# Ten of 22 up and gate pairs by seven block products in a fused two-block kernel

## The chip, the cores and the metric

The kernel runs on one core of a Trainium2 chip. The metric is the time of one execution on the device in microseconds (us); the profiler's trace of one execution shows where the time goes.

## What is computed

Two network blocks run one after the other on 512 tokens of width 1024, all in float32. The change lies in the last part, the gated feed-forward network of the second block:

```python
def conv_gated_mlp(xn, w_up_gate, conv_w_ffn, w_down):
    u, g = jnp.split(xn @ w_up_gate, 2, axis=-1)      # w_up_gate: 1024 x 5632
    u = causal_dwconv_2(u, conv_w_ffn)                # 3 taps along the tokens
    return (jax.nn.gelu(u) * g) @ w_down              # w_down: 2816 x 1024
...
        ffn = conv_gated_mlp(rms_norm(h, g_pre_ffn[layer]), w_up_gate[layer],
                             conv_w_ffn[layer], w_down[layer])
        h = h + rms_norm(ffn, g_post_ffn[layer])
```

Sixteen meta tokens stand ahead of the 512. The convolution reaches back two tokens, so u is made for 516 columns (four of them ahead of the 512).

## The kernel before

Matrix products are done in a split form: every float32 operand becomes a rounded part hi (type fp32r) and the rest lo = x - hi, and a product of two 128-deep blocks is three matmuls, hi·hi, hi·lo and lo·hi (`mm3`, L101 to L103). `split` (L77, L78) makes both parts: ScalarE casts to hi, VectorE subtracts. `load_w` (L87) brings one 1024x128 column block of a weight into a raw tile (three buffers, one DMA of 512 KB on SyncE's queue), and `split_w` splits it into `whi` and `wlo` (three buffers). `proj` multiplies one such block with half of the columns of x (258 of 516) over KT = 8 blocks of depth: 24 matmuls into one PSUM bank. Six banks go round for this.

The up projection works through 22 pairs m. A pair is one column block of u (weights at m·128) and the matching one of the gate (weights at 2816 + m·128), each for two halves of the columns: 4 calls of `proj`, 96 matmuls. x is here the residual h times the gain, not yet normed: the factor 1/rms of each token, `rb`, is multiplied in when PSUM is read (VectorE, L1269 for u, L1279 for the gate). Then the three taps of the convolution (VectorE, L1271 and twice L1273), the gelu (ScalarE, L1275) and the product with the gate (GpSimd, L1280) give `act[m]`. In pairs 6 to 13 one eighth of the residual each is loaded (L1255), transposed on TensorE (L1258) and copied to `ht` by VectorE (L1260); in pair 14 the gain `gpb` is loaded (L1284).

Ahead of it ends the mixer: its last projection into `yo`, `post_norm` (L266, L270), which adds to h, and `make_xs` (L82, L207), which makes the split x, `xs`, in two halves of columns; h lies in tiles of the ring `yc`. Behind it the down projection splits `act[k]` and the rows of w_down and runs 24 matmuls of 512 columns for each of 22 k into all eight banks.

Each engine has one queue and works it in order. What stands in it first is not set by the code's order alone: a planner sorts the instructions of each engine by a simulated time when the program is built, and a buffer that is taken again waits for its last reader. Pools with `reuse_waits="tile"` wait tile by tile for the memory of a released pool.

## Time and profile before

| | us |
|---|---|
| median of 3 runs | 1978.87 (1978.68 to 1979.2) |
| profiled execution, its own time | 1978.26 |
| its span in the trace | 1976.5 |
| up projection in the trace | 1584 to 1848 |
| mean granted clock of TensorE, of full speed | 0.998 |

The span is from the first to the last recorded instruction; about 1.8 us lie around it. PE is TensorE (matmuls; PEld its weight loads), DVE VectorE, ACT ScalarE, POOL GpSimd, SP SyncE, whose queue SPq issues the DMAs. Matmuls are pipelined: a recorded matmul lasts longer than the distance to the next, so the number of matmuls in a stretch, or the distance of two evictions, tells more than the busy time. In square brackets behind a row stands the idle time of the engine before it and what ended it.

### The profile page before, as it was taken

To read this page: it belongs to the slowest core of one execution; us is meant where nothing else is said; L and a number is where in the kernel's file an instruction comes from. 1 tells how busy PE (TensorE), PEld (TensorE's weight loads), DVE (VectorE), ACT (ScalarE), POOL (GpSimd) and SP (SyncE) were. 2 spreads that over 40 slices of the span, in tenths; PEclk is the share of its full clock that TensorE was granted. 3 is DMA by queue.
4 is the path that set the end of the run, shared out by engine and by line. 5 is a ranking of instruction groups with operands and counts; after the bars stand their busy time and mean duration, and the time that the engine had idled before them with its cause. 6 is when DMAs were issued, how large, how long until landed. Compare 5 with 4: busy or idle time off the path is not lost.

```text
span 1976.5 us, 33284 instructions
## 1 busy us (share of the span) xinstructions
PE 1953.6 (99%) x13398; PEld 1800.3 (91%) x13398; DVE 1267.4 (64%) x2143; ACT 973.5 (49%) x1839; POOL 246.1 (12%) x315
## 2 busy tenths in 40 slices
PE   8999999999999999999999999999999999999998
PEld 6999988888899888888899999999999999999886
DVE  6667677778672566664897878787344485655533
ACT  5555567768655633354756555555222452222322
POOL 1111000000030011100531212120001031111000
PEclk9999999999999999999999999999999999999999
DMA  6223322222433333333221222222333443332332
GB/s 179 67 79 88 86 76 75 75 65 86 144 110 106 95 89 89 92 133 118 88 65 55 65 65 65 58 68 81 92 94 93 149 126 99 102 102 86 96 96 75
DMA packets 260665, 181.37 MB, mean 92 GB/s; under 512 B 8866, under 2 KB 245631, under 8 KB 260511
## 3 DMA queue, kind: packets, MB, share of 16 engines
q1 hardware_dynamic: 259455, 179.21, 30.4%
q8 instruction: 105, 1.72, 0.4%
q14 instruction: 49, 0.40, 0.1%
q10 hardware_dynamic: 1056, 0.04, 0.0%
HBM read 168.59 MB, written 10.63 MB: 91 GB/s over the span
## 4 chain that ended last, share of the span: by engine, by line
PE 92%; DVE 4%; ACT 2%; POOL 1%; DMA 1%; issue 1%; DVEq 0%; POOLq 0%; ACTq 0%; SPq 0%
PE ps L103 17%; PE ps L101 17%; PE ps L102 17%; PE ps_v L103 5%; PE ps_v L102 5%; PE ps_v L101 5%; PE ps_o L101 3%; PE ps_o L102 3%; PE ps_o L103 3%; PE ps_d L101 2%; PE ps_d L103 2%; PE ps_d L102 2%; PE ps_z L1026 1%; PE ps_o L1103 1%; DVE yo L266 1%; DVE h L270 1%
## 5 line engine op out<-in xcount | busy, mean ns | idle before, releaser
L102 PE MATMUL ps<-xl,whi 128*128 128x258 f32 (+3 forms) x2112 | 656.0, 311 | 3.1 <-DVE xl L82 2.9
L101 PE MATMUL ps<-xh,whi 128*128 128x258 f32 (+3 forms) x2112 | 653.7, 313 | 1.0 <-ACT xh L81 0.9
L103 PE MATMUL ps<-xh,wlo 128*128 128x258 f32 (+3 forms) x2112 | 654.8, 311 | 0.0
L77 ACT CAST whi<-wraw 128x1024 fp32r<-128x1024 f32 (+2 forms) x315 | 314.5, 1004 | 454.1 <-PE ps L102 263.4
L78 DVE TENSOR_TENSOR wlo<-wraw,whi 128x1024 fp32r<-128x1024 f32 (+2 forms) x315 | 390.5, 1245 | 183.5 <-ACT whi L77 181.8
L102 PEld LDWEIGHTS ps<-xl,whi 128*128 128x128 f32 x2112 | 400.0, 189 | 28.0 <-DVE xl L82 4.9
L101 PEld LDWEIGHTS ps<-xh,whi 128*128 128x128 f32 x2112 | 397.3, 189 | 24.8 <-ACT xh L81 1.7
L103 PEld LDWEIGHTS ps<-xh,wlo 128*128 128x128 f32 x2112 | 399.3, 189 | 22.2
L101 PE MATMUL ps_v<-whi,xh 128*128 128x256 f32 x896 | 254.5, 286 | 3.5 <-ACT xh L81 3.1
L103 PE MATMUL ps_v<-whi,xl 128*128 128x256 f32 x896 | 253.6, 285 | 1.4 <-DVE xl L82 1.1
L102 PE MATMUL ps_v<-wlo,xh 128*128 128x256 f32 x896 | 254.1, 284 | 0.0
L101 PEld LDWEIGHTS ps_v<-whi,xh 128*128 128x128 f32 x896 | 169.6, 190 | 6.3 <-ACT xh L81 4.6
L103 PEld LDWEIGHTS ps_v<-whi,xl 128*128 128x128 f32 x896 | 170.0, 190 | 3.4 <-DVE xl L82 2.6
L102 PEld LDWEIGHTS ps_v<-wlo,xh 128*128 128x128 f32 x896 | 170.5, 190 | 1.5 <-DVE wlo L78 0.2
L103 PE MATMUL ps<-hi,wlo 128*128 128x258 f32 x384 | 108.7, 284 | 0.0
L101 PE MATMUL ps<-hi,whi 128*128 128x258 f32 x384 | 107.7, 282 | 0.0
L102 PE MATMUL ps_o<-xl,whi 128*128 128x512 f32 x192 | 75.7, 394 | 0.0
L101 PE MATMUL ps_o<-xh,whi 128*128 128x512 f32 x192 | 75.3, 395 | 0.0
L103 PE MATMUL ps_o<-xh,wlo 128*128 128x512 f32 x192 | 74.3, 394 | 0.0
L103 PEld LDWEIGHTS ps<-hi,wlo 128*128 128x128 f32 x384 | 72.7, 189 | 0.0
L101 PEld LDWEIGHTS ps<-hi,whi 128*128 128x128 f32 x384 | 72.4, 189 | 0.0
L103 PE MATMUL ps_d<-whi,xl 128*128 128x512 f32 x176 | 69.3, 394 | 0.0
(533 smaller groups left out, 3427.7 us busy)
## 6 DMA issues: line engine op xcount, KB each, us to landing
wraw<-in_l_w_in_dram SPq DMA_DIRECT2D x112, 512.0 KB
wraw<-in_w_in_dram SPq DMA_DIRECT2D x64, 512.0 KB
wraw<-in_w_up_gate_dram SPq DMA_DIRECT2D x44, 512.0 KB
wraw<-in_l_w_out_dram SPq DMA_DIRECT2D x24, 512.0 KB
wraw<-in_w_down_dram SPq DMA_DIRECT2D x22, 512.0 KB
wraw<-in_l_w_out_dram SPq DMA_DIRECT2D x16, 256.0 KB
wraw<-in_w_proj_attn_dram SPq DMA_DIRECT2D x8, 512.0 KB
wraw<-in_w_proj_conv_dram SPq DMA_DIRECT2D x8, 512.0 KB
```

What stands on the lines that cost most here:

```text
L77: A.copy(hi, src)
L78: V.tensor_tensor(lo, src, hi.bitcast(F32), op=ALU.subtract)
L101: T.matmul(ps, lhsT=ah, rhs=bh, start=first, stop=False, **kw)
L102: T.matmul(ps, lhsT=ah, rhs=bl, start=False, stop=False, **kw)
L103: T.matmul(ps, lhsT=al, rhs=bh, start=False, stop=last, **kw)
L266: mult = (G if i % 4 == 3 else V).tensor_tensor(yo[i][:, c], yo[i][:, c], r[:, c], op=ALU.mult)
L270: add_ = V.tensor_tensor(hs, hs, yo[i][:, c], op=ALU.add)
L1026: T.matmul(ps, lhsT=m_, rhs=x_[:, c0:c0 + n], start=False, stop=False, **kw)
L1103: T.matmul(po[:, n0:], lhsT=l_[:, b, hh:hh + 2, :].rearrange("p a d -> p (a d)"), rhs=a_[r_][:, c0:c0 + S - n0], start=po_first[0], stop=F ...
```

## The change

For ten of the pairs 6 to 21 the four products (u and gate, two halves of the columns) are computed as one 2x2 block product by seven products: the depth is cut into two halves of 4 blocks (HK), the weights into u and gate, x into its two halves of columns. `seven_w` loads both raw weights and forms the sums of blocks on VectorE (`sa`, `sb`), splits r1 whole (products 1 and 2), `sb` (6 and 3), `sa` (5 and 7) and the second half of r2 (4). `seven_x` forms, once for all pairs, the blocks and sums of x; because sums over columns and depth can't be normed afterwards by one factor, x is normed first (`xn` = h · gain · rb), in four steps within the pairs 0 to 3. `seven` runs the products, lets some add onto the bank of an earlier one, copies partial sums out by ScalarE (`keep`) and evicts u and the gate on VectorE with the additions left. The six other pairs of 6 to 21 are `plain`, with splits of the same normed x, u copied out by ScalarE, the gate multiplied with the gelu as it is evicted. The order from pair 6 on is SSPSSPSPSSPSSPSP (S by seven products). Pairs 0 to 5 stay as they were.

With it: the first tap of the convolution goes to ScalarE in all pairs; the product of gate and gelu goes from GpSimd to VectorE in the seven-product pairs; the copies of the residual go to ScalarE and into freed tiles of `xs`, in pairs 8 to 15; h gets tiles of its own (`hr`); `gpb` and the last splits of w_down are in a pool (`fd`) over the memory of the normed x, and gpb is loaded behind pair 21.

```diff
...
         T.matmul(ps, lhsT=ah, rhs=bh, start=first, stop=False, **kw)
         T.matmul(ps, lhsT=ah, rhs=bl, start=False, stop=False, **kw)
         T.matmul(ps, lhsT=al, rhs=bh, start=False, stop=last, **kw)
+    HK = KT // 2
+    kw = dict(skip_group_check=True)
+    def seven_w(pool, w, c1, c2):
+        lo, hi = slice(0, HK), slice(HK, KT)
+        r1 = load_w(w, 0, KT, c1, 128)
+        r2 = load_w(w, 0, KT, c2, 128)
+        sb = pool.tile([128, KT, 128], F32, tag="sb", name="sb", bufs=1)
+        sa = pool.tile([128, KT, 128], F32, tag="sa", name="sa", bufs=1)
+        w_ = {}
+        def put(names, *sp_):
+            for i, nm in enumerate(names):
+                w_[nm] = [x_[:, i * HK:(i + 1) * HK] for x_ in sp_]
+        put("12", *split_w(r1))
+        V.tensor_tensor(sa[:, lo], r2[:, lo], r2[:, hi], op=ALU.add)
+        V.tensor_tensor(sb[:, lo], sa[:, lo], r1[:, lo], op=ALU.add)
+        V.tensor_tensor(sb[:, hi], sb[:, lo], r1[:, hi], op=ALU.add)
+        put("63", *split_w(sb))
+        V.tensor_tensor(sa[:, hi], r1[:, lo], r2[:, lo], op=ALU.add)
+        put("57", *split_w(sa))
+        four = [pool.tile([128, HK, 128], F32R, tag=f"four{r}", name="four", bufs=1) for r in "hl"]
+        split(r2[:, hi], *four)
+        put("4", *four)
+        return w_
+    def seven_x(pool, tmp, p, xa, xb, n, out):
+        tq = tmp.tile([128, 4, n], F32, tag="tq", name="tq", bufs=2)
+        h0, h1 = slice(0, n), slice(n, 2 * n)
+        t1, t2, t3, t4 = (tq[:, i] for i in range(4))
+        V.tensor_tensor(t1, xa[:, h0], xa[:, h1], op=ALU.subtract)
+        V.tensor_tensor(t3, xa[:, h1], xb[:, h1], op=ALU.subtract)
+        V.scalar_tensor_tensor(t2, xb[:, h1], -1.0, t1, op0=ALU.mult, op1=ALU.subtract)
+        V.tensor_tensor(t4, xb[:, h0], t2, op=ALU.add)
+        for src, names in ((xa, "10"), (xb, "23"), (tq.rearrange("p a b -> p (a b)"), "5674")):
+            sp_ = [pool.tile([128, n * len(names)], F32R, tag=f"sx{names}{r}{p}", name=f"sx{r}") for r in "hl"]
+            split(src, *sp_)
+            for i, nm in enumerate(names):
+                out[nm, p] = [x_[:, i * n:(i + 1) * n] for x_ in sp_]
+    def seven(sw, sx, n, snap, o11, o12, o21, o22):
+        bank = {}
+        def product(nm, b, start):
+            if start:
+                bank[b] = pst("mm", n, f"ps_s{b}")
+            wh, wl = sw[nm]
+            for k in range(HK):
+                mm3(bank[b], wh[:, k], wl[:, k], *sx[nm, k], start and k == 0, k == HK - 1, **kw)
+            return bank[b]
+        def keep(ps):
+            t_ = next(snap)
+            A.copy(t_, ps)
+            return t_
+        s1 = keep(product("1", "x", True))
+        V.tensor_tensor(o11, product("2", "y", True), s1, op=ALU.add)
+        v2 = keep(product("6", "x", False))
+        s7 = keep(product("7", "w", True))
+        x5 = product("5", "x", False)
+        v4 = keep(x5)
+        n22, n21 = o22.shape[1], o21.shape[1]
+        V.tensor_tensor(o22, s7[:, n - n22:], x5[:, n - n22:], op=ALU.subtract)
+        V.tensor_tensor(o12, product("3", "z", True), v4, op=ALU.add)
+        V.tensor_tensor(o21, product("4", "w", False)[:, n - n21:], v2[:, n - n21:], op=ALU.subtract)
+    def plain(wt, sx, n, half, c0=0):
+        ps = pst("mm", n - c0)
+        wh, wl = wt
+        for k in range(KT):
+            xh, xl = sx[("10", "23")[k // HK][half], k % HK]
+            mm3(ps, wh[:, k, :], wl[:, k, :], xh[:, c0:], xl[:, c0:], k == 0, k == KT - 1)
+        return ps
     def w_cols(w, c0, n, fine=None):
...
         mo = tc.alloc_tile_pool(name="mo", bufs=1, reuse_waits="tile")
         mg = list(split_into("of", part))
         yo = [mx.tile([128, NQ], F32, tag=f"part{i}", name=f"yo{i}") for i in range(KT)]
-        h[:] = [ring("yc") for i in range(KT)]
+        hr = tc.alloc_tile_pool(name="hr", bufs=1, side="right", reuse_waits="tile")
+        h[:] = [hr.tile([128, NQ], F32, tag=f"h{i}", name=f"h{i}") for i in range(KT)]
         for i in range(KT):
             nc.sync.dma_start(h[i], hd[i][:, Q0:])
         acc, acc2 = new_acc(), new_acc()
...
     banks(mm=(2, 3, 4, 5, 6, 7), at=(0, 1))
     load_set(SET_GELU, "bc")
     with ExitStack() as ff:
-        fp = ff.enter_context(tc.tile_pool(name="fp", bufs=2))
-        act = [fp.tile([128, S], F32, tag=f"act{i}", name=f"act{i}", bufs=1) for i in range(22)]
-        gpb = fp.tile([128, D], F32, tag="gpb", name="gpb", bufs=1)
-
-        ht = [fp.tile([128, D], F32, tag=f"ht{t}", name=f"ht{t}", bufs=1) for t in range(4)]
+        fp = ff.enter_context(tc.tile_pool(name="fp", bufs=2, reuse_waits="tile"))
+        FIRST = 6
+        act = [fp.tile([128, S], F32, tag=f"act{i}", name=f"act{i}", bufs=1) for i in range(FIRST)]
+        wu = a["w_up_gate_2"][0]
+        def conv_gelu(m, u):
+            cv = fp.tile([128, S], F32, tag="cv", name="cv")
+            A.activation(cv, u[:, 4:], AF.Copy, scale=pv("conv_w_ffn_2", 44 + m))
+            for tp in (1, 2):
+                V.scalar_tensor_tensor(cv, u[:, 4 - tp:NQ - tp], pv("conv_w_ffn_2", (2 - tp) * 22 + m), cv,
+                                       op0=ALU.mult, op1=ALU.add)
+            last["gelu"] = A.activation(cv, cv, AF.Gelu_apprx_tanh)
+            return cv
+        fx = tc.alloc_tile_pool(name="fx", bufs=1, reuse_waits="tile")
+        ft = tc.alloc_tile_pool(name="ft", bufs=1, side="right", reuse_waits="tile")
+        sx = {}
+        for m in range(FIRST):
+            wt = split_w(load_w(wu, 0, KT, m * 128, 128))
+            u = fp.tile([128, NQ], F32, tag="u", name="u")
+            for i in range(2):
+                ps = proj(wt, xs, i * HQ, HQ)
+                V.tensor_tensor(u[:, i * HQ:(i + 1) * HQ], ps, rb[:, i * HQ:(i + 1) * HQ], op=ALU.mult)
+            cv = conv_gelu(m, u)
+            wt = split_w(load_w(wu, 0, KT, FF + m * 128, 128), parts=1 if m else 4)
+            for c0, c1 in ((4, HQ), (HQ, NQ)):
+                ps = proj(wt, xs, c0, c1 - c0)
+                V.tensor_tensor(act[m][:, c0 - 4:c1 - 4], ps, rb[:, c0:c1], op=ALU.mult)
+            G.tensor_tensor(act[m], act[m], cv, op=ALU.mult)
+            xn = []
+            for i in (m, m + HK) if m < HK else ():
+                xn.append(ft.tile([128, NQ], F32, tag="xn", name="xn", bufs=2))
+                V.scalar_tensor_tensor(xn[-1], h[i], pv("g_pre_ffn_2", i), rb[:, :NQ], op0=ALU.mult, op1=ALU.mult)
+            if xn:
+                seven_x(fx, ft, m, *xn, HQ, sx)
+        ft.release()
+        hr.release()
+        fa = tc.alloc_tile_pool(name="fa", bufs=1, side="right", reuse_waits="tile")
+        act += [fa.tile([128, S], F32, tag=f"act{i}", name=f"act{i}") for i in range(FIRST, 22)]
+        fw = tc.alloc_tile_pool(name="fw", bufs=1, side="right", reuse_waits="tile")
+        free = [xsp.tile([128, L2], F32, tag="xs", name="fr") for _ in range(16)]
+        ht = [[free[2 * t + i][:, :S] for i in range(2)] for t in range(4)]
+        hls = itertools.cycle([x_[:, :S] for x_ in free[8:10]])
+        snap = itertools.cycle([x_[:, c:c + HQ] for x_ in free[10:] for c in (0, HQ)])
         def residual(i):
-            hl = fp.tile([128, S], F32, tag="hl", name="hl")
+            hl = next(hls)
             nc.sync.dma_start(hl, hd[i][:, META:])
             ps = pst("at", S, "ps_h")
             for t in range(4):
                 T.transpose(ps[:, t * 128:(t + 1) * 128], hl[:, t * 128:(t + 1) * 128], ident)
             for t in range(4):
-                V.tensor_copy(ht[t][:, i * 128:(i + 1) * 128], ps[:, t * 128:(t + 1) * 128])
-
-        wu = a["w_up_gate_2"][0]
-        uw, gw = w_cols(wu, 0, FF), w_cols(wu, FF, FF, 1)
-        for m in range(22):
-            wt = next(uw)
+                A.copy(ht[t][i // 4][:, i % 4 * 128:(i % 4 + 1) * 128], ps[:, t * 128:(t + 1) * 128])
+        for m in range(FIRST, 22):
             u = fp.tile([128, NQ], F32, tag="u", name="u")
-            for i in range(2):
-                ps = proj(wt, xs, i * HQ, HQ)
-                V.tensor_tensor(u[:, i * HQ:(i + 1) * HQ], ps, rb[:, i * HQ:(i + 1) * HQ], op=ALU.mult)
-            cv = fp.tile([128, S], F32, tag="cv", name="cv")
-            V.tensor_scalar(cv, u[:, 4:], pv("conv_w_ffn_2", 44 + m), None, op0=ALU.mult)
-            for tp in (1, 2):
-                V.scalar_tensor_tensor(cv, u[:, 4 - tp:NQ - tp], pv("conv_w_ffn_2", (2 - tp) * 22 + m), cv,
-                                       op0=ALU.mult, op1=ALU.add)
-            last["gelu"] = A.activation(cv, cv, AF.Gelu_apprx_tanh)
-            wt = next(gw)
-            for c0, c1 in ((4, HQ), (HQ, NQ)):
-                ps = proj(wt, xs, c0, c1 - c0)
-                V.tensor_tensor(act[m][:, c0 - 4:c1 - 4], ps, rb[:, c0:c1], op=ALU.mult)
-            G.tensor_tensor(act[m], act[m], cv, op=ALU.mult)
-            if 6 <= m < 14:
-                residual(m - 6)
-            elif m == 14:
-                nc.sync.dma_start(gpb, a["g_post_ffn_2"].to_broadcast([128, D]))
+            if "SSPSSPSPSSPSSPSP"[m - FIRST] == "S":
+                sw = seven_w(fw, wu, m * 128, FF + m * 128)
+                seven(sw, sx, HQ, snap, u[:, :HQ], u[:, HQ:], act[m][:, :HQ - 4], act[m][:, HQ - 4:])
+                cv = conv_gelu(m, u)
+                V.tensor_tensor(act[m], act[m], cv, op=ALU.mult)
+            else:
+                wt = split_w(load_w(wu, 0, KT, m * 128, 128))
+                for i in range(2):
+                    A.copy(u[:, i * HQ:(i + 1) * HQ], plain(wt, sx, HQ, i))
+                cv = conv_gelu(m, u)
+                wt = split_w(load_w(wu, 0, KT, FF + m * 128, 128))
+                for i, c in enumerate((slice(0, HQ - 4), slice(HQ - 4, S))):
+                    V.tensor_tensor(act[m][:, c], plain(wt, sx, HQ, i, 0 if i else 4), cv[:, c], op=ALU.mult)
+            if 8 <= m < 16:
+                residual(m - 8)
+        fw.release()
+        fx.release()
         load_set(SET_LN_EXP, "gelu")
         wd = a["w_down_2"][0]
         pss = [[pp.tile([128, S], F32, tag=f"b{(2 + 2 * t + i) % 8}", name="ps_d") for i in range(2)] for t in range(4)]
...
                 mm3(pss[t][i], ah[:, t * 128:(t + 1) * 128], al[:, t * 128:(t + 1) * 128], wh[:, cs], wl[:, cs],
                     k == 0, k == 21)
+        fd = ff.enter_context(tc.tile_pool(name="fd", bufs=2, reuse_waits="tile"))
+        gpb = fd.tile([128, D], F32, tag="gpb", name="gpb", bufs=1)
+        nc.sync.dma_start(gpb, a["g_post_ffn_2"].to_broadcast([128, D]))
         held = []
         for k in range(22):
             raw = load_w(wd, k, 1, 0, 1024)
-            wh, wl = (x_[:, 0, :] for x_ in (split_w(raw) if k < 18 else split_w(raw, fp, f"l{k % 2}")))
+            wh, wl = (x_[:, 0, :] for x_ in (split_w(raw) if k < 18 else split_w(raw, fd, f"l{k % 2}")))
             ah, al = (x_[:, :S] for x_ in new_xs())
             split(act[k], ah, al)
             if k < 18:
...
```

## Rows read from the trace of the kernel before

**Rows 1.** Page, parts 1 and 4: busy time by engine; the chain's shares.
```profile
PE 1953.6 (99%) x13398; PEld 1800.3 (91%) x13398; DVE 1267.4 (64%) x2143; ACT 973.5 (49%) x1839; POOL 246.1 (12%) x315
...
PE 92%; DVE 4%; ACT 2%; POOL 1%; DMA 1%; issue 1%; DVEq 0%; POOLq 0%; ACTq 0%; SPq 0%
```

**Rows 2.** Stretches: each engine's busy us, instructions; granted clock, DMA share, GB/s.
```profile
1584.00:1594.00 10.00, 7.67 (x56) 6.80 (x55) 9.93 (x18) 5.90 (x15) 7.29 (x8) 1.00 0.23 76
1594.00:1600.00 6.00, 5.51 (x32) 5.30 (x33) 5.76 (x13) 3.45 (x9) 2.09 (x4) 0.72 0.27 89
1607.30:1620.00 12.70, 12.70 (x106) 12.54 (x105) 10.84 (x25) 6.83 (x12) 1.61 (x2) 1.00 0.83 227
1607.30:1660.00 52.70, 52.70 (x441) 52.55 (x440) 36.26 (x60) 17.87 (x24) 7.33 (x6) 1.00 0.46 131
...
1800.00:1840.00 40.00, 40.00 (x336) 40.00 (x335) 22.41 (x31) 9.88 (x11) 5.20 (x4) 1.00 0.30 92
```

**Rows 3.** VectorE by time, pairs of the up projection: start, duration, line.
```profile
1632.44 0.43 DVE L1269 TENSOR_TENSOR u<-ps,rbc 128x258 f32<-128x258 f32 x1 [2.46 <-PE ps L103]
...
1633.45 1.23 DVE L78 TENSOR_TENSOR wlo<-wraw,whi 128x1024 fp32r<-128x1024 f32 x1
...
1639.18 1.94 DVE L78 TENSOR_TENSOR wlo<-wraw,whi 128x1024 fp32r<-128x1024 f32 x1 [0.58 <-ACT whi L77]
...
1643.93 0.43 DVE L1269 TENSOR_TENSOR u<-ps,rbc 128x258 f32<-128x258 f32 x1 [2.46 <-PE ps L103]
```

**Rows 4.** GpSimd by time, one multiplication of the up projection.
```profile
1638.74 1.30 POOL L1280 TENSOR_TENSOR act<-act,cv 128x512 f32<-128x512 f32 x1 [8.70 <-DVE act L1279]
```

**Rows 5.** Groups, shapes apart, up projection: count | busy us, mean ns | idle.
```profile
L78 DVE TENSOR_TENSOR wlo<-wraw,whi 128x1024 fp32r<-128x1024 f32 x42 | 63.6, 1516 | 7.3 <-ACT whi L77 7.2
...
L77 ACT CAST whi<-wraw 128x1024 fp32r<-128x1024 f32 x42 | 44.0, 1050 | 115.1 <-PE ps L102 110.9 <-issue 4.2
L1273 DVE SCALAR_TENSOR_TENSOR cv<-u,pcol,cv 128x512 f32<-128x512 f32 x43 | 31.8, 744 | 0.0
...
L1269 DVE TENSOR_TENSOR u<-ps,rbc 128x258 f32<-128x258 f32 x44 | 18.7, 425 | 50.3 <-PE ps L103 49.8 <-DMA hd<-yc 0.5
L1275 ACT ACTIVATE cv<-cv 128x512 f32<-128x512 f32 x21 | 13.3, 632 | 59.2 <-DVE cv L1273 59.2
L1271 DVE TENSOR_SCALAR cv<-u,pcol 128x512 f32<-128x512 f32 x22 | 10.6, 486 | 2.4 <-DVE u L1269 0.5
...
L1260 DVE COPY ht<-ps_h 128x128 f32<-128x128 f32 x32 | 7.0, 282 | 0.1
```

**Rows 6.** The same view, shapes together, end of the mixer to the down projection.
```profile
L256 ACT ACTIVATE yo<-ps,pcol 128x258 f32<-128x258 f32 x16 | 7.6, 474 | 14.1 <-PE ps L103 14.1
```

**Rows 7.** VectorE in order of time, around the start of the up projection.
```profile
1586.55 0.42 DVE L266 TENSOR_TENSOR yo<-yo,rbc 128x258 f32<-128x258 f32 x1
...
1606.25 0.63 DVE L82 SCALAR_TENSOR_TENSOR xl<-yc,pcol,xh 128x258 fp32r<-128x258 f32 x1 [0.22 <-ACT xh L81]
...
1620.82 2.00 DVE L78 TENSOR_TENSOR wlo<-wraw,whi 128x1024 fp32r<-128x1024 f32 x1 [0.54 <-ACT whi L77]
1622.74 0.68 DVE L78 TENSOR_TENSOR xl<-act,xh 128x512 fp32r<-128x512 f32 x1
```

**Rows 8.** ScalarE in order of time, the cast of pair 3's up weights.
```profile
1619.73 1.05 ACT L77 CAST whi<-wraw 128x1024 fp32r<-128x1024 f32 x1 [1.12 <-PE ps L102]
```

**Rows 9.** TensorE in order of time, where the second half of x came late.
```profile
1593.84 0.39 PE L102 MATMUL ps<-xl,whi 128*128 128x258 f32 x1 [1.46 <-DVE xl L82]
...
1597.71 0.42 PE L102 MATMUL ps<-xl,whi 128*128 128x258 f32 x1
1597.93 0.42 PE L103 MATMUL ps<-xh,wlo 128*128 128x258 f32 x1
```

**Rows 10.** SyncE's queue in order of time: DMA issues.
```profile
1607.30 0.92 SPq L1255 DMA_DIRECT2D hl<-hd  x2
1608.27 0.42 SPq L1284 DMA_DIRECT2D gpb<-in_g_post_ffn_dram  x1
```

More of the change, by code (lines that the diff above doesn't have):

```diff
@@ L278 @@
     HALVES = (slice(0, 256), slice(256, 512))
-    kw = dict(skip_group_check=True)
     def out_proj(w, y, new_y, hp, yo, acc, gname, groups, order, done, ahead=False):
@@ L1306 @@
         for t in range(4):
-            sq = fp.tile([128, S], F32, tag="sqd", name="sq")
-            ss = fp.tile([128, 3], F32, tag="ss", name="ss")
+            sq = fd.tile([128, S], F32, tag="sqd", name="sq")
+            ss = fd.tile([128, 3], F32, tag="ss", name="ss")
             og = [fp.tile([128, S], F32, tag=tag, name="og") for tag in ("u", "cv")]
@@ L1318 @@
                 cs = slice(i * 512, (i + 1) * 512)
-                V.scalar_tensor_tensor(og[i], og[i], ss[:, 2:3], ht[t][:, cs], op0=ALU.mult, op1=ALU.add)
+                V.scalar_tensor_tensor(og[i], og[i], ss[:, 2:3], ht[t][i], op0=ALU.mult, op1=ALU.add)
                 nc.sync.dma_start(out[0, t * 128:(t + 1) * 128, cs], og[i])
+        fa.release()
 _INS = [
```

## The prediction, written before the changed kernel was run

> **What bounds the kernel now.** I read the busy times first, then the chain, then the up projection by stretches, then its pairs on VectorE. TensorE is busy for 99% of the span and carries 92% of the chain that ended last; VectorE is at 64%, ScalarE at 49%, GpSimd at 12% [rows 1]. In the up projection itself TensorE holds 336 matmuls in 40 us with no gap, while VectorE is busy 22.4 of 40 us [rows 2]. So a matmul that is not issued is worth its whole pitch here, as long as VectorE, which pays for it, has the room. The pitch comes from two evictions of the second half of u, one pair apart: 1643.93 - 1632.44 = 11.49 us for 96 matmuls, 0.1197 us each [rows 3].
>
> The start of the stage is different. From 1584 to 1594 VectorE is busy 9.93 of 10 us with the norm that feeds x, and TensorE gets only 56 instructions in where 84 fit [rows 2]; the last piece of that x is made at 1606.25 [rows 7]. From 1607.3 to 1660, up to the end of pair 5, VectorE is busy 36.3 of 52.7 us, and in the first 12.7 of these 10.8 [rows 2].
>
> **The change part by part.** *Matmuls.* A pair costs 2 projections x 2 halves x 8 blocks x 3 = 96 matmuls. By seven products it is 7 x 4 x 3 = 84. Twelve less, times 0.1197, is 1.44 us; the columns are 258 instead of a mean of 257, which takes about 0.03 back. Ten pairs: **14.1 us** off TensorE. Weight loads, plain pairs and transposes keep their number.
>
> *VectorE in a seven-product pair.* It subtracts for 3.5 tiles of 128x1024 (r1, sb, sa, half of r2), adds four times over 128x512, evicts four times, runs two taps of the convolution and multiplies act by cv. A split alone takes 1.23 us (the row at 1633.45); the mean of all is 1.52, because one of two meets GpSimd's multiplication, 1.30 us from 1638.74, and then takes 1.94 [rows 3 to 5]. The change takes that multiplication off GpSimd from pair 6 on, so I use 1.23. The 128x512 add is not in the trace; the nearest rows are the 128x512 subtract, 0.68 [rows 7], and the 128x512 tap, 0.74 [rows 5], and I take 0.68 for it, for the half split and for the last multiplication. Sum: 3 x 1.23 + 0.68 + 4 x 0.68 + 4 x 0.425 + 2 x 0.744 + 0.68 = **11.0 us against 10.1 us of TensorE** (84 x 0.120). A plain pair costs VectorE 2 x 1.23 + 2 x 0.744 + 2 x 0.425 = 4.8 us against 11.5. Over the sixteen pairs that is 139 us against 170: VectorE fits, 82%, but only if it works ahead in the plain pairs for the seven-product ones.
>
> The Trainium skill, GPSIMD Engine Reference, section Key points, says that GpSimd shares its interfaces to SBUF with VectorE and that VectorE instructions with two inputs in SBUF contend with it. The 1.94 against 1.23 agrees. If the contention stayed, at the mean of 1.52, the pair would be 12.0 us, and the sixteen pairs 150 us, which is still under TensorE.
>
> *ScalarE in such a pair:* 3.5 casts of 1.05, four copies out of PSUM at 0.474 [rows 6], one tap and one gelu at about 0.63: 6.8 us of 10.1 [rows 5]. It is hidden, but its queue is in order: three of the copies stand between two products that share a bank (1 and 6, 6 and 5, 7 and 4). One whole product, 1.44 us, lies between for each, and a copy needs 0.47; a cast of 1.05 in front of it would make it 0.1 us late. Between nothing and 0.1 us each, up to 3 us in all; I take none.
>
> *Two seven-product pairs in a row* (four such places). There are three buffers for split weights and such a pair holds all three. The first pair's sb is read until its product 3, 8.6 us after its start. If the buffers come free in the order in which they were taken, the second pair's sb and sa can only be split from there: cast 1.05, subtract 1.23, subtract 1.23 and an add 0.68, and whatever of the first pair's two last evictions (0.85), taps (1.49) and multiplication (0.68) goes ahead, 4.2 to 7.2 us. The second pair's product 7, which needs sa, starts 10.1 + 4.3 - 8.6 = 5.8 us later. So a stall from none to 1.4 us at each of four places; the middle, 0.7, gives **2.8 us**.
>
> *The normed x, in pairs 0 to 3.* Each of four steps is two 128x516 products (0.744), four operations of 128x258 (0.42 [rows 7]), two splits of 516 (0.68) and one of 1032 (1.23): 5.8 us of VectorE, 23.2 in all, none of which may be later than the first product of pair 6. VectorE gives back six first taps that go to ScalarE (6 x 0.486) and four copies of the residual (4 x 0.282), 4.0 us [rows 5], and pair 6 needs three adds more ahead of its start (2.0). Demand from 1607.3 to the start of pair 6: 36.3 - 4.0 + 23.2 + 2.0 = 57.5 us. Time for it: 52.7 + 1 = 53.7. Without any loss of order 3.8 us are missing; the last pair's taps and gate evictions (2.3) can be put off, and waits between dependent operations cost some. From 1.5 us upward, then; I take **4 us**.
>
> *Costed at nothing:* h moves to tiles of its own, so that it lives until the normed x is made; its eight loads come earlier, beside full TensorE. The residual's copies go to ScalarE, which has room. gpb's load now needs the place of the normed x and so can't go before pair 21 is nearly done, with the down weights' loads behind it on SyncE's queue. But queues here are filled as work becomes ready, not as the code reads: in the trace this load goes out at 1608.27, while pair 2 is worked on, and its place in the code is pair 14 [rows 10]. Its cover is the three buffers of raw weights; if that is gone it costs one load (512 KB at 227 GB/s [rows 2], 2.3 us) and a cast and a split, 4.6 us.
>
> *Sum.* The profiled execution took 1978.26 us, 0.6 under the median of the runs. 1978.3 - 14.1 + 2.8 + 4 = 1971.0; with the 0.6, **1971.5 us**.
>
> **The rivals.** *All of it is kept.* The waits at the joins and the shortage before pair 6 are filled with other work; 1978.9 - 14.1 + 1.5 = 1966. For it: the order on VectorE is mixed freely, for instance a split of act for the down projection, whose place is behind pair 21, at 1622.74 among the work of pairs 2 and 3 [rows 7]. Against it: 57.5 us into 53.7.
>
> *The normed x goes ahead of the weights.* If ready work is taken in the order of the code, the x steps 0 to 2 (17.4 us) run before the split of pair 3's up weights, whose buffer is only free at 1619.73 [rows 8]. That split starts at 1620.82 [rows 7]; pair 3 starts at 1632.44 - 5.75 - 0.2 = 1626.5, so it may start 4.4 us later; about 1.9 us of VectorE's time before it were idle [rows 2]. TensorE then stops for 17.4 - 4.4 - 1.9 = 11 us, and nothing is short at pair 6: 1978.9 - 14.1 + 11 + 2.8 = 1978.6, no change. Such a stop has a second price: after the wait of 1.46 us that ended at 1593.84, and sparse work before it, the granted clock fell for a while to the lower level, 1.2 GHz, with matmuls 0.22 us apart [rows 9], a mean of 0.72 over 1594 to 1600 [rows 2]. That is about 1.5 us more, 1980. The Trainium skill, TensorE: Matmul & The Clock Gate, section Why this matters for your kernels, states it as a rule: idle gaps between bursts of matmuls put the clock back to half. By that rule this rival ends at 1980, without it at 1978.6; the trace bears it out.
>
> *VectorE can't work ahead (slower).* If the three weight buffers and the single sa, sb and four tiles keep VectorE from using the plain pairs, every seven-product pair pays what I put at the joins, 1.4 us, and three late copies at 0.1 besides, 1.7 x 10 = 17 us; with the 4 us at the start and 4.6 at gpb that is 1978.9 - 14.1 + 17 + 4 + 4.6 = 1990. It decides from (14.1 - 4) / 10 = 1.0 us of stall for each such pair on. For it: 11.0 us of VectorE against 10.1. Against it: the plain pair leaves 6.7 us of VectorE free, more than two seven-product pairs lack.
>
> **How the numbers follow.** The forecast, 1968 to 1975: 0.42. All kept, under 1968: 0.20. Normed x ahead, 1975 to 1983: 0.20. Slower, 1983 to 1995: 0.18. The range takes in the floor of the sum with a little below it and most of the two other cases: 1964.5 to 1985. About 0.2% (4 us) is what a measurement of this kernel can tell from no change: faster 0.62, same 0.20, slower 0.18.
>
> **What would show it.** Right: 120 matmuls fewer; two evictions of neighbouring seven-product pairs 10 to 11 us apart; VectorE above 90% from 1607 to the start of pair 6 and a short wait of TensorE there for the normed x. Wrong: TensorE idle at pair 3 for wlo (normed x ahead); waits in every seven-product pair for wlo or for a copy (slower); no waits at all (all kept); splits beside the adds longer than 1.23 us.

## The result, and the profile after

| kernel | median us | against the kernel before, 95% interval |
|---|---|---|
| before | 1978.78 (1978.39 to 1979.2) | |
| changed | 1965.53 (1965.45 to 1966.58) | 0.9936 (0.9923 to 0.9948) |

The change takes 13.25 us off, more than the 7.3 us of the forecast. The time lies inside the range of 1964.5 to 1985, close to its lower end; the case that came true is the one called "all of it is kept" (1966), not the likeliest one.

The page of the changed kernel, its parts 1 (busy us by engine, share of the span, instructions) and 4 (shares of the chain), answers to [rows 1]:

```profile
PE 1939.6 (99%) x13278; PEld 1784.5 (91%) x13278; DVE 1303.5 (66%) x2183; ACT 1033.8 (53%) x1977; POOL 231.4 (12%) x299
...
PE 91%; DVE 5%; ACT 2%; POOL 1%; DMA 1%; issue 1%; DVEq 0%; POOLq 0%; ACTq 0%; SPq 0%
```

TensorE has 13278 instructions where it had 13398: the 120 matmuls are gone. VectorE did not become the bound: it stands in 5% of the chain, ahead 4%. Its busy time grew by 36 us and GpSimd's fell by 15.

The stretches of the changed kernel (busy us and instructions of TensorE, its weight loads, VectorE, ScalarE and GpSimd; granted clock; DMA share; GB/s), against [rows 2]:

```profile
1607.30:1660.00 52.70, 52.16 (x432) 51.53 (x431) 51.06 (x80) 28.89 (x38) 10.80 (x6) 1.00 0.35 101
1660.00:1700.00 40.00, 40.00 (x335) 40.00 (x335) 34.83 (x49) 20.77 (x36) 3.61 (x1) 1.00 0.36 105
1700.00:1740.00 40.00, 40.00 (x338) 40.00 (x337) 26.17 (x38) 23.05 (x48) 0.00 (x0) 1.00 0.43 126
```

From 1607 to 1660 VectorE is busy 51.1 of 52.7 us, where it was 36.3. From 1660 to 1820 TensorE issues 335 to 338 instructions in each 40 us, as many as before (336), and no wait of TensorE is recorded between 1661.4 and 1831: the seven-product stage loses next to nothing. So the whole question is why the costs that the prediction put at the joins and at the start did not come.

### The profile page after: what moved, and what is told of

Its sections match the earlier page's. It is cut to its first block, busy times and chain, and to the rows that moved or that the text cites. A ratio compares the mean times of both kernels' runs of the same rounds, so it can differ in the third digit from the quotient of the medians.

```text
span 1963.7 us, 33145 instructions
## 1 busy us (share of the span) xinstructions
PE 1939.6 (99%) x13278; PEld 1784.5 (91%) x13278; DVE 1303.5 (66%) x2183; ACT 1033.8 (53%) x1977; POOL 231.4 (12%) x299
## 4 chain that ended last, share of the span: by engine, by line
PE 91%; DVE 5%; ACT 2%; POOL 1%; DMA 1%; issue 1%; DVEq 0%; POOLq 0%; ACTq 0%; SPq 0%
PE ps L101 15%; PE ps L103 15%; PE ps L102 15%; PE ps_v L102 5%; PE ps_v L101 5%; PE ps_v L103 5%; PE ps_o L101 3%; PE ps_o L102 3%; PE ps_o L103 3%; PE ps_d L101 2%; PE ps_d L103 2%; PE ps_d L102 2%; PE ps_z L1109 1%; PE ps_o L1186 1%; DVE xl L82 1%; DVE h L354 1%
## 5 line engine op out<-in xcount | busy, mean ns | idle before, releaser
L102 PE MATMUL ps<-xl,whi 128*128 128x258 f32 (+3 forms) x1600 | 511.1, 321 | 3.7 <-DVE xl L82 3.5
L101 PE MATMUL ps<-xh,whi 128*128 128x258 f32 (+3 forms) x1600 | 508.1, 322 | 1.1 <-ACT xh L81 0.4
L103 PE MATMUL ps<-xh,wlo 128*128 128x258 f32 (+3 forms) x1600 | 509.0, 320 | 0.0
L77 ACT CAST whi<-wraw 128x1024 fp32r<-128x1024 f32 (+2 forms) x305 | 304.3, 1003 | 368.9 <-PE ps L102 164.7
L78 DVE TENSOR_TENSOR wlo<-wraw,whi 128x1024 fp32r<-128x1024 f32 (+2 forms) x305 | 366.6, 1207 | 179.6 <-ACT whi L77 178.3
L102 PEld LDWEIGHTS ps<-xl,whi 128*128 128x128 f32 x1600 | 302.5, 189 | 28.8 <-DVE xl L82 5.5
L101 PEld LDWEIGHTS ps<-xh,whi 128*128 128x128 f32 x1600 | 300.2, 189 | 25.3 <-ACT whi L77 1.2
L103 PEld LDWEIGHTS ps<-xh,wlo 128*128 128x128 f32 x1600 | 301.7, 189 | 22.3
L101 PE MATMUL ps_d<-whi,xh 128*128 128x512 f32 x176 | 69.3, 394 | 0.0
```

Source lines behind the costliest of these rows:

```text
L77: A.copy(hi, src)
L78: V.tensor_tensor(lo, src, hi.bitcast(F32), op=ALU.subtract)
L101: T.matmul(ps, lhsT=ah, rhs=bh, start=first, stop=False, **kw)
L102: T.matmul(ps, lhsT=ah, rhs=bl, start=False, stop=False, **kw)
L103: T.matmul(ps, lhsT=al, rhs=bh, start=False, stop=last, **kw)
```

## The experiments

All times are medians, the ratios against runs of the kernel before on the same chip. The intervals of tap_vector and twelve overlap that of the changed kernel, and those of the three edits of all_seven overlap that of all_seven. The single executions of these kernels do not overlap where a difference is named below, but the argument rests on the traces too and not on the times alone.

| kernel | us | ratio (95%) |
|---|---|---|
| all_plain: no pair by seven products | 1979.73 | 1.0006 (0.9996 to 1.0015) |
| tap_vector: first tap on VectorE in pairs 0 to 5 | 1967.53 | 0.9948 (0.9933 to 0.9962) |
| first5: the stage one pair earlier | 1972.50 | 0.9969 (0.9956 to 0.9982) |
| ten_two_sa: changed kernel, two buffers for sa | 1965.87 | 0.9934 (0.9920 to 0.9949) |
| mult_gpsimd: product of gate and gelu on GpSimd | 1965.63 | 0.9933 (0.9918 to 0.9948) |
| twelve: 12 of 16 by seven products | 1963.38 | 0.9923 (0.9907 to 0.9940) |
| twelve_3_early | 1963.50 | 0.9922 (0.9906 to 0.9939) |
| all_seven: 16 of 16 | 1964.25 | 0.9928 (0.9913 to 0.9943) |
| seven_3_early | 1967.50 | 0.9943 (0.9928 to 0.9958) |
| seven_mult_gpsimd | 1960.87 | 0.9912 (0.9897 to 0.9927) |
| seven_two_sa | 1958.96 | 0.9902 (0.9886 to 0.9919) |
| seven_sa_gpsimd | 1967.38 | 0.9941 (0.9925 to 0.9958) |

### Where the gain comes from: no pair by seven products

```diff
-            if "SSPSSPSPSSPSSPSP"[m - FIRST] == "S":
+            if "PPPPPPPPPPPPPPPP"[m - FIRST] == "S":
```

> Pairs 6 to 21 all plain: the normed x, its sums and splits, the moved h, the copies and the first tap on ScalarE stay, and no pair uses seven products. If the gain is the matmuls that are not issued and nothing else, this gives it all back: ten pairs x 1.41 = 14.1 us more, 1979.6. If part of the gain came from the rest of the change (h in tiles of its own, work taken off VectorE and GpSimd), it stays below 1978; if the rest has a price that the seven-product pairs paid for, it is above 1981.

Measured: 1979.73. That is 14.2 us above the changed kernel, ten times 1.42, close to the price that the prediction put on twelve matmuls (1.41). The rest of the change together (normed x, moved h, work handed to ScalarE) costs between nothing and 1.2 us; the interval holds 1. So the gain comes with the matmuls that are not issued. Not all of the 14.2 lies in the stage itself, from the first matmul of pair 6 to the first of the down projection. The first row is the start of pair 6 in all_plain (in the changed kernel it is at 1661.50, below); the two others are the matmuls into `ps_d` (count, shortest, median and longest in ns, first and last start), in all_plain and in the changed kernel:

```profile
1662.30 0.28 PE L101 MATMUL ps<-sxh,whi 128*128 128x258 f32 x1
...
L101 PE MATMUL ps_d<-whi,xh x31: 388/394/398, 1848.9 to 1869.6; 128*128 128x512 f32 x31
L101 PE MATMUL ps_d<-whi,xh x51: 388/393/398, 1834.8 to 1869.5; 128*128 128x512 f32 x51
```

The stage takes 186.6 us without and 173.3 us with seven-product pairs, 13.3 us less, 1.33 for each. Pair 6 starts 0.8 us later in all_plain, which is nearly all of the rest.

### Is VectorE full up to pair 6?

```diff
-            A.activation(cv, u[:, 4:], AF.Copy, scale=pv("conv_w_ffn_2", 44 + m))
+            if m < FIRST:
+                V.tensor_scalar(cv, u[:, 4:], pv("conv_w_ffn_2", 44 + m), None, op0=ALU.mult)
+            else:
+                A.activation(cv, u[:, 4:], AF.Copy, scale=pv("conv_w_ffn_2", 44 + m))
```

> The first tap of the convolution back on VectorE in pairs 0 to 5 only. VectorE is then asked for 6 x 0.41 = 2.5 us more in the stretch where it is busy 97% of the time. If that stretch is full, TensorE waits there for most of it: 1967 to 1968. If there is slack (work that can be put off behind pair 6): 1965.5, no change.

Measured: 1967.53, 2.0 us more, of 2.5 that VectorE was asked for. The stretch behind the start of pair 6 in this kernel (columns as above) has 322 instructions on TensorE where the changed kernel has 335:

```profile
1660.00:1700.00 40.00, 39.12 (x322) 38.51 (x321) 34.36 (x49) 22.45 (x37) 3.18 (x2) 1.00 0.37 106
```

The second test moves the stage itself:

```diff
-        FIRST = 6
+        FIRST = 5
...
-            if "SSPSSPSPSSPSSPSP"[m - FIRST] == "S":
+            if "SSPSSPSPSSPSSPSPP"[m - FIRST] == "S":
```

> The seven-product stage begins one pair earlier: five pairs ahead of it instead of six, then SSPSSPSPSSPSSPSPP; still ten by seven products. The normed x has to be ready 11.5 us earlier, while only one ordinary pair's work (2 x 1.13 + 2 x 0.66 + 4 x 0.34 = 4.9 us by distances of starts) moves behind it. If VectorE is full up to pair 6, TensorE waits for the difference, 6.6 us, before the first seven-product pair: about 1972. If there was room left: 1965.5 to 1967.

Measured: 1972.50, 7.0 us more, where 6.6 were expected of a VectorE with no room. Its stretches, and then the waits of TensorE (for whom; us in total, times, longest) show the price where it was put: 23 instructions fewer than 432 up to 1660 and 30 fewer than 335 from there to 1700, about 6.3 us around the first seven-product pairs, for x, for weights and for copies at once.

```profile
1607.30:1660.00 52.70, 50.35 (x409) 49.11 (x409) 50.84 (x80) 27.92 (x39) 6.43 (x6) 1.00 0.33 94
1660.00:1700.00 40.00, 37.48 (x305) 36.65 (x305) 30.89 (x44) 20.58 (x34) 4.77 (x1) 1.00 0.35 100
```

```profile
PE ps_sx L101 <- ACT fr L166: 0.9, 2, 0.7
PE ps_sx L101 <- ACT whi L77: 0.8, 1, 0.8
PE ps_sx L101 <- ACT sxh L77: 0.7, 1, 0.7
```

Both say the same: up to pair 6 VectorE has hardly any time left, and in the changed kernel the work just fits.

### Are the joins of two seven-product pairs free?

```diff
-        sa = pool.tile([128, KT, 128], F32, tag="sa", name="sa", bufs=1)
+        sa = pool.tile([128, KT, 128], F32, tag="sa", name="sa", bufs=2)
```

> The changed kernel itself (ten by seven products, six plain) with two buffers for sa and nothing else. If its joins of two seven-product pairs are free, as its trace says, no change: 1965 to 1966. If they hide a wait of the 0.7 us each that the prediction put there, up to 2.8 us less: 1962.7 to 1964.

Measured: 1965.87, no change. With ten such pairs and plain ones between them there was no wait to take away.

```diff
-                V.tensor_tensor(act[m], act[m], cv, op=ALU.mult)
+                G.tensor_tensor(act[m], act[m], cv, op=ALU.mult)
```

> In the ten seven-product pairs the product of gate and gelu goes back to GpSimd. VectorE is asked for 0.60 us less a pair, but its operations beside GpSimd's get longer (a 1024 split went from 1.23 to 1.94 before). If VectorE's time decides there, the time moves by a microsecond or more, up or down; if the stage has room (82% by the sum), no change: 1965 to 1966.

Measured: 1965.63, no change: with room on VectorE it doesn't matter who multiplies. Nor did VectorE get lighter: from 1660 to 1820 it is busy 123.8 us, against 123.3 in the changed kernel, since operations beside GpSimd's took longer (the taps 0.89 us on average instead of 0.75).

### How far does it go: twelve and sixteen

The only edit of twelve is the order of pairs; all_seven has S sixteen times.

```diff
-            if "SSPSSPSPSSPSSPSP"[m - FIRST] == "S":
+            if "SSSPSSSPSSSPSSSP"[m - FIRST] == "S":
```

> Twelve seven-product pairs in groups of three, four plain. Theory A: two more pairs gained, 2 x 1.41 = 2.8 us, 1962.7. Theory B (three in a row lack 3 x 0.9 us of VectorE's time and a buffer at each join): 1964 to 1968.

Measured: 1963.38, 2.2 us less than the changed kernel where 2.8 were expected; the two intervals overlap. Most of the rest lies ahead of the stage: pair 6 starts at 1662.0 here and at 1661.5 in the changed kernel. In the kernels that share all code up to pair 6 this start lies between 1661.4 and 1662.4, so less than a microsecond between two of them says nothing.

> All sixteen pairs 6 to 21 by seven products, no plain pair between. Theory A (VectorE's instructions overlap: what counts is the distance of starts, 1.13 us for a 1024 subtract, 0.60 for 512, 0.34 for 258, 0.66 for a tap, in sum 9.7 us a pair against 10.1 of TensorE): TensorE stays the bound, 6 x 1.41 less, 1957 to 1959. Theory B (as predicted, durations of 11.0 us a pair): VectorE becomes the bound, 16 x 11.0 = 176 us where the stage now takes 170, 1970 to 1972.

Measured: 1964.25, between both. Six more pairs bring 1.3 us instead of 8.5. Pair 6 starts 0.8 us later than in the changed kernel, and up to 1740 TensorE still issues 335 instructions in each 40 us; the loss lies behind that. There it gets 314 and 304 instructions into 40 us instead of 336 (6.5 us), while VectorE is busy for 92%. The waits of VectorE and of TensorE (for whom; us, times, longest) are mostly for ScalarE's casts, and the largest of each is:

```profile
1740.00:1780.00 40.00, 38.70 (x314) 37.83 (x313) 37.02 (x58) 20.97 (x35) 0.00 (x0) 1.00 0.32 93
1780.00:1820.00 40.00, 37.92 (x304) 36.67 (x304) 36.46 (x56) 24.12 (x39) 0.00 (x0) 1.00 0.36 106
```

```profile
DVE wlo L78 <- ACT whi L77: 9.1, 8, 1.9
PE ps_sx L101 <- ACT whi L77: 2.3, 6, 0.6
```

So VectorE is neither idle nor full. Three edits of this kernel follow. The first moved product 3 ahead of product 7 in the code, to free sb sooner:

```diff
         v2 = keep(product("6", "x", False))
+        p3 = product("3", "z", True)
         s7 = keep(product("7", "w", True))
...
-        V.tensor_tensor(o12, product("3", "z", True), v4, op=ALU.add)
+        V.tensor_tensor(o12, p3, v4, op=ALU.add)
```

> All sixteen pairs by seven products, and product 3 moved ahead of product 7 (order 1, 2, 6, 3, 7, 5, 4), so that the split sb comes free after four products, 5.7 us into the pair and not 8.6, and sa after six. VectorE, ScalarE and TensorE do the same work. Theory A (all sixteen lost 7 of 8.5 us at the hand-over of the three weight buffers, not for want of VectorE's time): 1957 to 1960. Theory B (VectorE, busy for 92% there, is simply full): 1963.5 to 1965, no change against all sixteen in the old order (1964.25).

> Twelve seven-product pairs in threes, product 3 ahead of 7. In the old order TensorE had no recorded wait in these pairs, 1963.4. Theory A and B both: 1962.5 to 1963.5, since nothing waited there; if the order of the products has a price of its own (a bank held longer), above 1965.

Measured: 1967.50, 3.3 us slower than the old order, and 1963.50 with twelve, no change. The edit did not do what its expectation says. TensorE in order of time, in pair 7 of seven_3_early, runs product 7 (bank ps_sw) ahead of product 3 (ps_sz), although the code has them the other way round:

```profile
1675.19 0.28 PE L101 MATMUL ps_sw<-sxh,whi 128*128 128x258 f32 x1
...
1678.08 0.28 PE L101 MATMUL ps_sz<-sxh,whi 128*128 128x258 f32 x1
```

The planner sorts the products by its own simulated times. In seven_3_early it has 7 ahead of 3 in three of the sixteen pairs (7, 8 and 11); with the old code it had put 3 ahead of 7 in every pair already, in all_seven as in the changed kernel. So this run says nothing about the buffers, though the next expectation takes it so; why its order came out slower was not taken apart.

The second is all_seven with the multiplication of mult_gpsimd:

```diff
-                V.tensor_tensor(act[m], act[m], cv, op=ALU.mult)
+                G.tensor_tensor(act[m], act[m], cv, op=ALU.mult)
```

> All sixteen pairs by seven products (1964.25 so far), with the product of gate and gelu on GpSimd. Earlier freeing of sb did not help (1967.5), so theory A is down to this question: is VectorE's time short (theory B), or the chain cast, subtract, product (theory C)? VectorE gives up 0.60 us a pair and takes some back where its operations run beside GpSimd's 1.3. B: about half of the lost 7 us comes back, 1959 to 1962. C: no change or worse, 1964 to 1967.

Measured: 1960.87, 3.4 us less than all_seven, as theory B had it. Here VectorE does get lighter: between 1740 and 1820 it is busy 74.6 us for 660 instructions of TensorE, in all_seven 73.5 us for 618.

The third is all_seven with the two tiles of ten_two_sa:

```diff
-        sa = pool.tile([128, KT, 128], F32, tag="sa", name="sa", bufs=1)
+        sa = pool.tile([128, KT, 128], F32, tag="sa", name="sa", bufs=2)
```

> All sixteen pairs by seven products with two buffers for the sum tile sa instead of one, so that the next pair's sums can be formed before this pair's sa is split. VectorE's work is the same. Theory B (VectorE's time is short): 1963.5 to 1965, no change. Theory C (the sums wait for their single buffer and come late): 1958 to 1962.

Measured: 1958.96, 5.3 us less, with the same work on VectorE. The time is theory C's, but its cause, a wait for the single tile, isn't shown. VectorE at a hand-over, the split of this pair's sa and the next pair's first sum (L125), in all_seven (first two lines) and in seven_two_sa:

```profile
1761.26 1.21 DVE L78 TENSOR_TENSOR wlo<-sa,whi 128x1024 fp32r<-128x1024 f32 x1
...
1763.99 0.68 DVE L125 TENSOR_TENSOR sa<-wraw 128x512 f32<-128x512 f32 x1
...
1759.68 1.22 DVE L78 TENSOR_TENSOR wlo<-sa,whi 128x1024 fp32r<-128x1024 f32 x1
1760.82 0.69 DVE L125 TENSOR_TENSOR sa<-wraw 128x512 f32<-128x512 f32 x1
```

A sum ahead of the split, which only a second tile allows, occurs at one of the fifteen hand-overs. At the others L125 starts 1.1 to 2.4 us after the split's start, where all_seven has 2.1 to 3.3, with other work between. One tile allows that too: the changed kernel has 1.3 us at its joins. What the traces show is another order on VectorE, in which the sums come earlier; a kernel with this order and one tile was not run. In seven_mult_gpsimd the sums stand as in all_seven (2.1 to 3.4 us). So neither theory holds alone: less work for VectorE helps, and the order of the same work counts too. The stretches and VectorE's waits, to be read against those of all_seven:

```profile
1740.00:1780.00 40.00, 40.00 (x332) 39.75 (x331) 38.56 (x60) 22.96 (x39) 0.00 (x0) 1.00 0.35 104
1780.00:1820.00 40.00, 40.00 (x331) 39.84 (x331) 38.88 (x61) 22.99 (x40) 0.00 (x0) 1.00 0.35 101
```

```profile
DVE wlo L78 <- ACT whi L77: 4.3, 6, 1.6
```

TensorE is back at 332 and 331 instructions, VectorE at 97%, and its waits for casts fell from 9.1 to 4.3 us. These two stretches also give VectorE's price of a seven-product pair: (38.56 + 38.88) us for (332 + 331) / 84 = 7.9 pairs, 9.8 us each. All sixteen pairs with two tiles for sa is the fastest kernel here, faster than before (0.9902) and than the changed one (0.9936; the intervals don't meet).

Both edits together, the sa of two tiles and the multiplication on GpSimd:

> All sixteen by seven products, two buffers for sa, and the product of gate and gelu on GpSimd. With two buffers alone it was 1958.96, against 1957.0 for the matmuls alone (1965.5 - 6 x 1.41). If the 1.9 us left are VectorE's, busy 97% there, they go: 1957 to 1958. If they are the hand-over at the end of the stage or a wait on ScalarE: 1958.5 to 1960, no change.

Measured: 1967.38, 8.4 us slower than two tiles alone: a miss. The waits in its seven-product stage, and VectorE in order of time:

```profile
DVE sa L125 <- DMA wraw<-in_w_up_gate_dram: 17.5, 9, 2.8
...
PE ps_sw L101 <- DVE act L176: 4.0, 5, 1.5
```

```profile
1752.68 0.69 DVE L125 TENSOR_TENSOR sa<-wraw 128x512 f32<-128x512 f32 x1 [2.57 <-DMA wraw<-in_w_up_gate_dram]
...
1755.63 0.42 DVE L176 TENSOR_TENSOR act<-fr,ps_sx 128x258 f32<-128x258 f32 x1
```

At eight of the fifteen hand-overs VectorE's queue has the next pair's first sum (L125) ahead of this pair's split of sa, which the second tile allows, and here ahead of its evictions (L176) too. The sum waits 2.6 us for its raw weights to arrive, the eviction stands behind it, and TensorE waits for the bank: 17.5 us of VectorE's time in all, against 1.2 in seven_two_sa. With the multiplication off VectorE the planner pulled the sums forward into a wait for a load. There are three raw tiles; a fourth was not tried.

## Where the prediction held and where it didn't, point by point

Right were the bound and the direction, and the matmuls nearly to the size. The sum, 1971.5, was 6 us too high, since its two other terms hardly came; that the time lies in the range is owed to the range, which took in the case that all is kept. Of the signs for "right" three came: 120 matmuls fewer, evictions 10.1 us apart, VectorE at 97% up to pair 6. The fourth, a short wait of TensorE for the normed x, didn't, and the sign of "all kept", no waits, did.

**The matmuls** came out nearly as put: 14.1 us expected, 14.2 between all_plain and the changed kernel, 13.3 of it within the stage.

**VectorE's price of a seven-product pair** was mis-sized: 11.0 us expected, 9.8 measured. The sum added recorded durations. VectorE in order of time in the changed kernel shows what is wrong with that:

```profile
1665.27 0.41 DVE L170 TENSOR_TENSOR u<-ps_sy,fr 128x258 f32<-128x258 f32 x1
...
1672.67 1.22 DVE L78 TENSOR_TENSOR wlo<-sa,whi 128x1024 fp32r<-128x1024 f32 x1
1673.80 0.42 DVE L176 TENSOR_TENSOR act<-fr,ps_sx 128x258 f32<-128x258 f32 x1
...
1675.40 0.42 DVE L170 TENSOR_TENSOR u<-ps_sy,fr 128x258 f32<-128x258 f32 x1
...
1682.61 0.69 DVE L125 TENSOR_TENSOR sa<-wraw 128x512 f32<-128x512 f32 x1 [2.16 <-DMA wraw<-in_w_up_gate_dram]
1683.21 0.69 DVE L129 TENSOR_TENSOR sa<-wraw 128x512 f32<-128x512 f32 x1
1683.82 0.69 DVE L126 TENSOR_TENSOR sb<-sa,wraw 128x512 f32<-128x512 f32 x1
1684.54 0.69 DVE L127 TENSOR_TENSOR sb<-sb,wraw 128x512 f32<-128x512 f32 x1
1685.15 1.22 DVE L78 TENSOR_TENSOR wlo<-wraw,whi 128x1024 fp32r<-128x1024 f32 x1
1686.28 0.42 DVE L176 TENSOR_TENSOR act<-fr,ps_sx 128x258 f32<-128x258 f32 x1
1686.62 0.42 DVE L177 TENSOR_TENSOR u<-ps_sz,fr 128x258 f32<-128x258 f32 x1
```

The rows at 1672.67 and 1673.80 are the split of pair 7's sa and an eviction of pair 6; they are needed below. A 128x512 sum lasts 0.69 us and the next begins 0.60 to 0.61 us after its start (0.72 where it reads the sum just before it, at 1684.54); 1024 take 1.22 and 1.13, 258 take 0.42 and 0.34. Back to back, each instruction costs about 0.08 us less than its row says. With 15 of them in a pair that is 1.2 us, the whole difference. The Trainium skill, Perfetto Trace Analysis, section Per-engine timelines, gives a reason: the reported window of such an instruction runs to the acknowledgement of its last write, while the next may begin its prefetch when the arithmetic is done. The trace agrees. The unknown add was sized well, 0.68 against 0.69. With 9.8 us VectorE's share of the sixteen pairs is (10 x 9.8 + 6 x 4.8) / 170 = 75% and not 82% (in the trace 123.3 of 160 us, 77%), and below TensorE's 10.1 in each single pair; that is what the rival "VectorE can't work ahead" rested on. Two neighbouring pairs' first evictions (L170) lie 10.1 us apart, as the prediction asked for.

**The joins** were costed at 2.8 us and cost none. The prediction had the second pair's sa ready 12.8 to 15.8 us after the first pair's start (8.6 until sb comes free, then 4.2 to 7.2) and needed at 14.4. The step that failed is the assumed order, on TensorE and on VectorE. On TensorE the prediction took the products in the order of the code, 1, 2, 6, 7, 5, 3, 4, and one pair after the other. TensorE in order of time, pairs 6 and 7 (products 1, 6 and 5 go to bank ps_sx, 2 to ps_sy, 3 to ps_sz, 7 and 4 to ps_sw):

```profile
1661.50 0.28 PE L101 MATMUL ps_sx<-sxh,whi 128*128 128x258 f32 x1
...
1671.39 0.28 PE L101 MATMUL ps_sw<-sxh,four 128*128 128x258 f32 x1
...
1674.53 0.28 PE L101 MATMUL ps_sz<-sxh,whi 128*128 128x258 f32 x1
...
1677.41 0.28 PE L101 MATMUL ps_sw<-sxh,whi 128*128 128x258 f32 x1
```

Product 4 of pair 6 starts at 1671.39, 9.9 us after the pair's start, where six products take 8.6: matmuls of pair 7 have been put ahead of it. Product 3 stands ahead of product 7 in all ten pairs; in pair 7 it starts at 1674.53 and product 7 at 1677.41, where the prediction's order would have had product 7 at 1661.5 + 10.1 + 4.3 = 1675.9.

On VectorE none of the first pair's last evictions, taps and multiplication goes ahead of the second pair's splits: sa's subtract runs from 1672.67 to 1673.9, and pair 6's eviction L176 comes behind it (above). So sa is ready 12.4 us after pair 6's start, under the low end of the estimate. That leaves 3.5 us of slack, and 2.0 even if product 7 had come at 1675.9. ScalarE in order of time at this join and at the next (pairs 9 and 10), and VectorE's split at the next:

```profile
1670.44 1.05 ACT L77 CAST whi<-sb 128x1024 fp32r<-128x1024 f32 x1 [1.38 <-DVE sb L127]
...
1703.85 1.05 ACT L77 CAST whi<-sa 128x1024 fp32r<-128x1024 f32 x1 [1.03 <-PE ps_sx L102]
...
1704.93 1.23 DVE L78 TENSOR_TENSOR wlo<-sa,whi 128x1024 fp32r<-128x1024 f32 x1 [1.52 <-ACT whi L77]
```

In pair 7 the cast of sb waited for VectorE's sum (L127) and no buffer. At the three other joins the cast of sa did wait for TensorE to let go of a buffer, 0.5 to 1.0 us, as the prediction has it, but with 2.9 to 4.1 us to spare before product 7. The prediction's own bound from below, none, was the right end.

**The start** was costed at 4 us. VectorE is indeed full there, the mechanism that was named: 51.1 of 52.7 us, and first5 pays 7.0 of 6.6 us expected. But the demand was too high by the same overlap: it added 39 operations by their durations and took ten off, and at 0.08 us each that is 2.3 of the 3.8 us that seemed to be missing. The 1.5 left are less than the 2.3 that could be put off. VectorE in order of time, once around pair 3's weights and once around the start of pair 6, whose first matmul is at 1661.50:

```profile
1621.73 1.21 DVE L78 TENSOR_TENSOR wlo<-wraw,whi 128x1024 fp32r<-128x1024 f32 x1
...
1623.20 0.41 DVE L145 TENSOR_TENSOR tq<-xn,tq 128x258 f32<-128x258 f32 x1
...
1625.93 1.21 DVE L78 TENSOR_TENSOR wlo<-wraw,whi 128x1024 fp32r<-128x1024 f32 x1
...
1661.34 1.21 DVE L78 TENSOR_TENSOR wlo<-sb,whi 128x1024 fp32r<-128x1024 f32 x1
1662.47 0.74 DVE L1341 SCALAR_TENSOR_TENSOR cv<-u,pcol,cv 128x512 f32<-128x512 f32 x1
...
1663.47 1.21 DVE L78 TENSOR_TENSOR wlo<-sa,whi 128x1024 fp32r<-128x1024 f32 x1
```

The split of sb begins with pair 6, that of sa and two taps of pair 5 (the second at 1664.61) run behind its start; the first product that reads sb comes two products later. What is left is read from the start of pair 6. In the kernel before, the last eviction of pair 5 is at

```profile
1661.13 0.43 DVE L1279 TENSOR_TENSOR act<-ps,rbc 128x258 f32<-128x258 f32 x1 [1.81 <-PE ps L103]
```

and pair 6 begins about 0.2 us ahead of it, at 1660.9. In the changed kernel it begins at 1661.5: 0.6 us, where 4 were put.

The rows around pair 3 answer the rival **"the normed x goes ahead of the weights"**. Splits of weights (1621.73, 1625.93) stand between the pieces of tq: ready work was mixed, and the stop of 11 us at pair 3 did not come. TensorE's only recorded wait between 1607 and 1661.5 is 0.4 us, for a cast of weights.

**Costed at nothing, and so it was:** gpb's load. SyncE's queue in order of time:

```profile
1807.51 24.38 SPq L87 DMA_DIRECT2D wraw<-in_w_down_dram  x5
1832.53 0.33 SPq L1418 DMA_DIRECT2D gpb<-in_g_post_ffn_dram  x1
```

It went out at 1832.53, when the normed x was nearly done with, behind five loads of the down projection's weights and not ahead of them, and no wait of TensorE is recorded from 1820 to the end. The copies on ScalarE were hidden too, at 0.374 us each instead of the 0.474 taken; between products 7 and 4 lie two products and not one, so that copy has more room than the prediction gave it.

**The three terms of the sum**, then: -14.1 is -13.3 in the stage, +2.8 for the joins is none, and +4 for the start is 0.6. That makes -12.7, where the spans of the two traces differ by 12.8.

## What to carry to other kernels

Where one engine is the bound and another is at two thirds, trading matmuls for vector work pays nearly the full pitch of each matmul (here 13.3 of 14.1 us), up to the point at which the helper's queue is full; that point has to be found by the distance of starts in a packed stretch, not by adding durations. Near it the order in that queue decides and not the sum of work alone: one more buffer for an intermediate sum gave 5.3 us, mostly without being used as a second buffer, and taking work off the full engine gave 3.4 alone and cost 8.4 together with that buffer; with the buffer the planner's order had changed both times. So an edit in a planned program has to be checked in the trace for the order that it really made.

## What was not expected of the hardware

GpSimd pays for a full VectorE as VectorE pays for GpSimd. One of its multiplications of 128x512, and an operation of VectorE beside it, in order of time in the changed kernel:

```profile
1646.08 4.82 POOL L1360 TENSOR_TENSOR act<-act,cv 128x512 f32<-128x512 f32 x1 [10.20 <-ACT cv L1343]
...
1650.00 1.19 DVE L143 TENSOR_TENSOR tq<-xn 128x258 f32<-128x258 f32 x1
```

The six multiplications take 1.30, 1.46, 1.32, 4.82, 1.31 and 3.61 us. VectorE's queue is packed beside each of them; why two are long is not shown. VectorE pays once each time, however long GpSimd takes: beside each of the six, one of its operations is 0.8 to 1.1 us longer than its kind, as the row at 1650.00 with 1.19 us where 258 elements take 0.42 elsewhere. The Trainium skill, GPSIMD Engine Reference, section Key points, names the shared interfaces; that the slower engine can take 3.7 times as long is this trace's. It did not matter here, since nobody waited for act.
